# Token-half steps and a scaling product at the two layer ends of a fused two-block kernel

## The chip, the cores and the metric

The kernel runs on one core of one Trainium2 chip. The metric is the device time of one execution in microseconds (us), over 3 runs of the same program. A profiled execution of it gives the trace from which all rows below come; times in rows count from the start of its span.

## What is computed

Two transformer-like blocks run one after the other on 256 tokens of width 2048, in fp32. The parts that matter here are the ends of the two sublayers of the first block: a product with a wide weight, a normalisation over each token's whole row, a residual sum, and a second normalisation whose result feeds the next product.

```python
def rmsnorm(x, g):
    y = xf * lax.rsqrt(jnp.mean(xf * xf, axis=-1, keepdims=True) + RMS_EPS)
    return (y * g.astype(jnp.float32)).astype(x.dtype)

# first_block
x = x + gt_a * rmsnorm(mix @ w_out[l], g_post_attn[l])          # layer end 1
h = rmsnorm(x, g_pre_ffn[l]) * (1.0 + sc_f) + sh_f
f = (jax.nn.silu(h @ w_gate[l]) * (h @ w_up[l])) @ w_down[l]
x = x + gt_f * rmsnorm(f, g_post_ffn[l])                        # layer end 2

# second_block
h = rms_norm(x, norm1_w[l]) * (1.0 + scale[:, None, :]) + shift[:, None, :]
proj = h @ w_in[l] + b_in[l]                                    # begins with v
```

## The kernel before

**Steps.** All wide products are cut into steps of one 128x2048 weight tile (1 MB): SP loads it (`raw`, a ring of 4 buffers), ACT rounds it to `hi` (L243), DVE subtracts (`lo`, L244), and PE multiplies. An fp32 product is three products of rounded parts (L325 to L327), so a step is 4 chunks of 128 input features x 3 products x 2 token halves = 24 matmuls of 128x512. The activations are the stationary side, kept as `khi` and `klo` for each token half `th` (128 tokens). Four steps (`kq` 0 to 3) make one 512-wide output group. `hi` and `lo` have 2 buffers each; an "early" step takes eight 128x512 tiles of the 40-buffer pool `kp` instead, and a "fine" step is converted in 4 or 8 pieces, so that it can start sooner. `run_steps` converts the weights of one step ahead of the step that multiplies.

**Layer end.** The steps of layer end 1 are `wo` (groups `g` 0 to 3), those of layer end 2 the last quarter of the down-projection `dn` (column groups `cg` 0 to 3, two steps each). Each group ends with `z_out`: ACT squares the product and sums it (`jz`, L719), DVE multiplies by a row of gains (L722). That row comes from `row_bcast`: ACT makes eight 128x128 diagonal tiles `dg` (L346), two matmuls spread them over the partitions (`row<-dg,onesr`, L354), DVE multiplies by the gain. After the last group `post_add` takes the root (L330, L331), adds to x (L758), squares again (L760) and takes the second root `r2`. `norm_quad` then handles 128 tokens x 512 features: x is scaled by `r2` (`xs`, L768 on ACT or L770 on DVE), transposed in four PE products against `ident` (`xn`, L773), scaled and shifted per feature (`hn`, L778 and L780, DVE and ACT in turn), and split to `khi` and `klo` (L301, L302). There are 8 quads: 4 for each token half.

**What overlaps.** The last two steps before the end are held and then run token half by token half (24 matmuls of half 0, then 24 of half 1), so the chain of half 0 can run under half 1. The first two steps of the next layer (`gu` after layer end 1, `v` after layer end 2) are held in the same way (`first_steps`); its steps 2 and 3 run both halves together. The engines issue in the order of the program that a scheduler wrote at build time, each engine in order.

Of the kernel before, what the change touches and what calls it, by code (L numbers as in the profile page):

```python
# [12 lines left out]
AF = mybir.ActivationFunctionType  # L13
# [76 lines left out]
def build(tc, A, out):  # L90
# [123 lines left out]
    def run_steps():  # L214
# [3 lines left out]
        fine = {i + d: n for i in barriers for d, n in ((0, 4), (2, 8), (3, 4))}  # L218
        early = {i + 1 for i in barriers}
# [27 lines left out]
        for i in range(n):  # L247
            cur[0] = i
            prep(i)
            prep(i + 1)  # L250
            _, _, fn, _, fill_n, post = steps[i]
            fill(fill_n)
            hi, lo = prepped.pop(i)
            fn(hi, lo)
            for f in pending.pop(i, []):
                f()
            if post is not None:
                post()
# [26 lines left out]
    def group_step(dsts, hi, lo, K, k0, q, nq, last):  # L285
        ks = range(k0 + 4 * q, k0 + 4 * q + 4)
        if last and q == nq - 2:
            held.append((hi, lo))
        elif last and q == nq - 1:
            hi0, lo0 = held.pop()  # L290
            for th in range(2):
                group_mm(dsts, hi0, lo0, K, range(k0 + 4 * q - 4, k0 + 4 * q), nq == 2, False, (th,))
                group_mm(dsts, hi, lo, K, ks, False, True, (th,))
        else:
            group_mm(dsts, hi, lo, K, ks, q == 0, q == nq - 1)
# [255 lines left out]
    MIX = {}  # L551
# [177 lines left out]

    def wo_step(g, kq):  # L730
        def fn(hi, lo):
# [7 lines left out]
            group_step(gacc[g], hi, lo, MIX, 0, kq, 4, g == 3)  # L739
            if kq == 3:  # L740
                p = gacc.pop(g)
                for th in range(2):
                    z_out(g, th, p[th])
# [19 lines left out]

    def norm_quad(th, q, K):
        xs = ttile("xs")
        src = x[:, th, 512 * q:512 * q + 512]
        if q % 2:
            act.activation(xs, src, AF.Copy, scale=r2[:, th:th + 1])  # L768
        else:
            dve.tensor_scalar(xs, src, r2[:, th:th + 1], None, op0=OP.mult)  # L770
        p = at_tile("xn")
        for i in range(4):
            pe.transpose(p[:, i * 128:(i + 1) * 128], xs[:, i * 128:(i + 1) * 128], ident)  # L773
# [9 lines left out]
    def barrier(K):  # L783

        post_add(0)
        norm_quad(0, 0, K)
        norm_quad(0, 1, K)
        post_add(1)

    def first_steps(K, kq, dsts, hi, lo):  # L790

        if kq == 0:
            held.append((hi, lo))
        elif kq == 1:
            ws = [held.pop(), (hi, lo)]
            for th in range(2):
                if th:
                    norm_quad(1, 0, K)
                    norm_quad(1, 1, K)
                for q, (h, l) in enumerate(ws):  # L800
                    group_mm(dsts, h, l, K, range(4 * q, 4 * q + 4), q == 0, False, (th,))
            norm_quad(0, 2, K)
            norm_quad(1, 2, K)
        else:
            group_mm(dsts, hi, lo, K, range(4 * kq, 4 * kq + 4), False, kq == 3)
            if kq == 2:
                norm_quad(0, 3, K)
                norm_quad(1, 3, K)
# [56 lines left out]
    def dn_step(g, cg, q):  # L865
        nq = FGRP[g] // 4

        def fn(hi, lo):
# [9 lines left out]
            group_step(gacc[0], hi, lo, FF, fbase[g], q, nq, g == NG - 1 and cg == 3)  # L878
            if q == nq - 1:
                p = gacc.pop(0)  # L880
                for th in range(2):
# [5 lines left out]
                    if g == NG - 1:  # L887
                        z_out(cg, th, Z[cg, th])
                if g == NG - 1 and cg == 2:
                    preload_sqrt(ssz[:, 2:3])  # L890
# [369 lines left out]
    def wo2_step(g, kq):  # L1260
        def fn(hi, lo):
# [5 lines left out]
            group_step(gacc[g], hi, lo, MG, 0, kq, 4, g == 3)  # L1267
# [123 lines left out]
```

## Time and profile before

| what | us |
|---|---|
| three runs, median (lowest to highest) | 2493.19 (2492.52 to 2494.2) |
| the profiled execution, its time | 2494.39 |
| its span in the trace | 2492.6 |
| PE busy in it | 2415.2 (97%) |
| DVE busy | 1584.0 (64%) |
| ACT busy | 1152.5 (46%) |
| mean granted clock of TensorE | 0.986 of full |

The profiled execution is 1.2 us above the median of the runs. Busy time of PE counts a matmul as long as it occupies the engine, at either of its two clocks, 1.2 and 2.4 GHz (granted 0.5 and 1.00); what PE loses is idle time plus the time at the lower clock.

### The profile page before, as it was taken

How to read it: one execution, taken by the hardware profiler on the slowest of the kernel's cores; microseconds unless marked ns; L12 is line 12 of the kernel's file. 1: busy time of each engine (PE TensorE's matmuls, PEld its weight loads, DVE VectorE, ACT ScalarE, POOL GpSimd, SP SyncE). 2: the span in 40 equal slices, each digit the busy share in tenths (PEclk: the TensorE clock that was granted, in tenths of full speed). 3: DMA queues.
4: the chain of work that ended last, by engine and by line, in shares of the span. 5: the costliest groups of instructions: out<-in, count | busy, mean ns of one | idle time of the engine just before them, and what ended most of it. 6: DMA issues, size and time to landing. Idle time of an engine off the chain costs nothing.

```text
span 2492.6 us, 30211 instructions
## 1 busy us (share of the span) xinstructions
PE 2415.2 (97%) x12444; PEld 2024.2 (81%) x12444; DVE 1584.0 (64%) x1702; ACT 1152.5 (46%) x1394; POOL 0.2 (0%) x4
## 2 busy tenths in 40 slices
PE   6999999979999999999979999999999999999998
PEld 4888888868888888888858888888888888888887
DVE  4888888766666566666664555565456566554555
ACT  5433887553343433334453335455333344344344
POOL 0000000000000000000000000000000000000000
PEclk9999989989999999999989999999999999999999
DMA  8987779937777777677635554555566677555553
GB/s 319 334 334 275 308 282 353 336 126 281 291 271 271 256 284 288 254 284 284 222 122 196 180 195 176 186 177 188 188 213 237 245 250 258 204 200 199 191 195 134
DMA packets 90434, 597.34 MB, mean 240 GB/s; under 512 B 10164, under 2 KB 10804, under 8 KB 20664
## 3 DMA queue, kind: packets, MB, share of 16 engines
q1 hardware_dynamic: 90296, 595.41, 66.0%
q8 instruction: 97, 1.59, 0.3%
q14 instruction: 41, 0.34, 0.0%
HBM read 593.28 MB, written 2.10 MB: 239 GB/s over the span
## 4 chain that ended last, share of the span: by engine, by line
PE 91%; ACT 4%; DVE 3%; DMA 2%; issue 1%; SPq 0%; ACTq 0%; DVEq 0%
PE gu L325 6%; PE gu L326 6%; PE gu L327 6%; PE dn L326 3%; PE dn L327 3%; PE dn L325 3%; PE v L325 2%; PE wo L326 2%; PE wo L325 2%; PE wo L327 2%; PE v L326 2%; PE v L327 2%; DMA graw<-i_ada_k 1%; PE z_a L325 1%; PE ga L325 1%; PE ga L327 1%
## 5 line engine op out<-in xcount | busy, mean ns | idle before, releaser
L244 DVE TENSOR_TENSOR lo<-raw,hi 128x2048 fp32r<-128x2048 f32 (+3 forms) x437 | 927.0, 2124 | 740.2 <-ACT hi L243 739.9
L243 ACT ACTIVATE hi<-raw 128x2048 fp32r<-128x2048 f32 (+3 forms) x437 | 776.9, 1782 | 1057.5 <-PE gu L327 261.1
L325 PE MATMUL gu<-hi,khi 128*128 128x512 f32 x696 | 272.8, 392 | 0.9 <-ACT khi L301 0.9
L326 PE MATMUL gu<-lo,khi 128*128 128x512 f32 x696 | 271.9, 391 | 0.0
L327 PE MATMUL gu<-hi,klo 128*128 128x512 f32 x696 | 271.8, 391 | 0.0
L172 DVE SCALAR_TENSOR_TENSOR graw<-graw,cb 128x2048 f32<-128x2048 f32 x112 | 256.0, 2285 | 16.0 <-DMA graw<-i_w_ada 11.3
L325 PEld LDWEIGHTS gu<-hi,khi 128*128 128x128 f32 x696 | 131.3, 189 | 28.3 <-ACT khi L301 1.1
L327 PEld LDWEIGHTS gu<-hi,klo 128*128 128x128 f32 x696 | 131.3, 189 | 27.5 <-DVE klo L302 0.2
L326 PEld LDWEIGHTS gu<-lo,khi 128*128 128x128 f32 x696 | 131.4, 189 | 27.1
L326 PE MATMUL dn<-lo,khi 128*128 128x512 f32 x352 | 137.3, 390 | 0.2 <-DVE lo L244 0.2
L327 PE MATMUL dn<-hi,klo 128*128 128x512 f32 x352 | 137.0, 389 | 0.0
L325 PE MATMUL dn<-hi,khi 128*128 128x512 f32 x352 | 136.6, 390 | 0.0
L326 PEld LDWEIGHTS dn<-lo,khi 128*128 128x128 f32 x352 | 66.1, 188 | 14.6 <-DVE lo L244 1.0
L325 PEld LDWEIGHTS dn<-hi,khi 128*128 128x128 f32 x352 | 66.1, 188 | 13.8
L327 PEld LDWEIGHTS dn<-hi,klo 128*128 128x128 f32 x352 | 66.1, 188 | 13.7
L281 PE MATMUL qk<-h,lo 128*128 128x256 f32 x256 | 74.1, 290 | 3.1 <-DVE lo L244 3.1
L279 PE MATMUL qk<-h,hi 128*128 128x256 f32 x256 | 75.2, 294 | 0.1
L513 PE MATMUL e<-h,lo 128*128 128x256 f32 x256 | 72.8, 288 | 1.8 <-DVE lo L244 1.8
L511 PE MATMUL e<-h,hi 128*128 128x256 f32 x256 | 73.9, 289 | 0.3 <-ACT gvs L197 0.3
L280 PE MATMUL qk<-h,hi 128*128 128x256 f32 x256 | 73.9, 289 | 0.0
L512 PE MATMUL e<-h,hi 128*128 128x256 f32 x256 | 72.9, 286 | 0.0
L281 PEld LDWEIGHTS qk<-h,lo 128*128 128x128 f32 x256 | 50.6, 197 | 3.5 <-DVE lo L244 3.5
(428 smaller groups left out, 4933.4 us busy)
## 6 DMA issues: line engine op xcount, KB each, us to landing
raw<-i_w_gu SPq DMA_DIRECT2D x88, 1024.0 KB, 4.8
graw<-i_ada_t SPq DMA_DIRECT2D x64, 1024.0 KB, 6.3
graw<-i_w_ada SPq DMA_DIRECT2D x48, 1024.0 KB, 4.8
raw<-i_w_dn SPq DMA_DIRECT2D x44, 1024.0 KB, 4.9
graw<-i_ada_k SPq DMA_DIRECT2D x32, 1024.0 KB, 6.9
raw<-i_w_out SPq DMA_DIRECT2D x32, 1024.0 KB, 4.9
raw<-i_w_s SPq DMA_DIRECT2D x24, 1024.0 KB, 6.8
raw<-i_w_qk SPq DMA_DIRECT2D x16, 1024.0 KB, 7.3
```

Source lines behind the costliest of these rows:

```text
L172: dve.scalar_tensor_tensor(g, g, 1.0, cb, op0=OP.mult, op1=OP.mult, accum_out=dst)
L243: act.activation(hi[:, b:e], r[:, b:e], AF.Copy)
L244: dve.tensor_sub(lo[:, b:e], r[:, b:e], hi[:, b:e].bitcast(F32))
L279: pe.matmul(dst, wh, K[k][:, 0, :], start=s, stop=False)
L280: pe.matmul(dst, wh, K[k][:, 1, :], start=False, stop=False)
L281: pe.matmul(dst, wl, K[k][:, 0, :], start=False, stop=e)
L325: pe.matmul(dsts[th], xh, wh, start=s, stop=False)
L326: pe.matmul(dsts[th], xh, wl, start=False, stop=False)
L327: pe.matmul(dsts[th], xl, wh, start=False, stop=e)
L511: pe.matmul(dst, hv[:, i, c0:c0 + 128], H[k][:, 0, :], start=(k == k0), stop=False)
L512: pe.matmul(dst, hv[:, i, c0:c0 + 128], H[k][:, 1, :], start=False, stop=False)
L513: pe.matmul(dst, lv[:, i, c0:c0 + 128], H[k][:, 0, :], start=False, stop=(k == k1 - 1))
```

## The change

At both layer ends more steps are held and run token half by token half: three before layer end 1 (`wo` group 3, `kq` 1 to 3) and four before layer end 2 (`cg` 2 and 3 of `dn`, two steps each), where it was two; and the first three steps of the next layer, where it was two. More of them are "early" or "fine" to have all their weights at hand, and a new set `late` moves the conversion of the next layer's fourth step behind the products of the third. `row_bcast` stays at the same place in the code, ahead of the step's products, which now are appended to a list there. The scaling by `r2` and the transposing become one product: x itself is the stationary side, and `dx`, the identity scaled by `r2` (one 128x128 DVE instruction for each token half), the moving one, in plain fp32. Three quads of each half run ahead of the first products, the fourth of both halves after them.

```diff
         n = len(steps)
         prepped = {}
         barriers = {i for i, st in enumerate(steps) if st[5] in (barrier1, barrier2)}
-        fine = {i + d: n for i in barriers for d, n in ((0, 4), (2, 8), (3, 4))}
-        early = {i + 1 for i in barriers}
+        fine = {i + d: n for i in barriers for d, n in ((-1, 4), (0, 4), (2, 8), (3, 8))}
+        early = {i + d for i in barriers for d in (-2, 1, 4)}
+        early |= {i - 3 for i, st in enumerate(steps) if st[5] is barrier2}
+        late = {i + 4 for i in barriers}
 
         def prep(i):
             if i >= n or i in prepped:
@@ -247,11 +249,13 @@
...
         for i in range(n):
             cur[0] = i
             prep(i)
-            prep(i + 1)
+            if i + 1 not in late:
+                prep(i + 1)
             _, _, fn, _, fill_n, post = steps[i]
             fill(fill_n)
             hi, lo = prepped.pop(i)
             fn(hi, lo)
+            prep(i + 1)
...
-    def group_step(dsts, hi, lo, K, k0, q, nq, last):
-        ks = range(k0 + 4 * q, k0 + 4 * q + 4)
-        if last and q == nq - 2:
-            held.append((hi, lo))
-        elif last and q == nq - 1:
-            hi0, lo0 = held.pop()
-            for th in range(2):
-                group_mm(dsts, hi0, lo0, K, range(k0 + 4 * q - 4, k0 + 4 * q), nq == 2, False, (th,))
-                group_mm(dsts, hi, lo, K, ks, False, True, (th,))
-        else:
-            group_mm(dsts, hi, lo, K, ks, q == 0, q == nq - 1)
+    def run_held(th):
+        for e in held:
+            group_mm(*e, ths=(th,))
...
-            group_step(gacc[g], hi, lo, MIX, 0, kq, 4, g == 3)
+            e = (gacc[g], hi, lo, MIX, range(4 * kq, 4 * kq + 4), kq == 0, kq == 3)
+            if g == 3 and kq:
+                held.append(e)
+            else:
+                group_mm(*e)
             if kq == 3:
                 p = gacc.pop(g)
+                if g == 3:
+                    run_held(0)
+                    run_held(1)
+                    held.clear()
+                    evac[0] = lambda th: z_out(g, th, p[th])
+                    return
...
+    DX = {}
+
     def norm_quad(th, q, K):
-        xs = ttile("xs")
-        src = x[:, th, 512 * q:512 * q + 512]
-        if q % 2:
-            act.activation(xs, src, AF.Copy, scale=r2[:, th:th + 1])
-        else:
-            dve.tensor_scalar(xs, src, r2[:, th:th + 1], None, op0=OP.mult)
         p = at_tile("xn")
         for i in range(4):
-            pe.transpose(p[:, i * 128:(i + 1) * 128], xs[:, i * 128:(i + 1) * 128], ident)
+            j = 4 * q + i
+            pe.matmul(p[:, i * 128:(i + 1) * 128], x[:, th, j * 128:(j + 1) * 128], DX[th], start=True, stop=True)
...
-        post_add(0)
-        norm_quad(0, 0, K)
-        norm_quad(0, 1, K)
-        post_add(1)
+        for th in range(2):
+            evac[0](th)
+            post_add(th)
+            DX[th] = ttile("dx")[:, 0:128]
+            dve.tensor_scalar(DX[th], ident, r2[:, th:th + 1], None, op0=OP.mult)
+            if th == 0:
+                for q in range(3):
+                    norm_quad(0, q, K)
 
     def first_steps(K, kq, dsts, hi, lo):
 
-        if kq == 0:
-            held.append((hi, lo))
-        elif kq == 1:
-            ws = [held.pop(), (hi, lo)]
-            for th in range(2):
-                if th:
-                    norm_quad(1, 0, K)
-                    norm_quad(1, 1, K)
-                for q, (h, l) in enumerate(ws):
-                    group_mm(dsts, h, l, K, range(4 * q, 4 * q + 4), q == 0, False, (th,))
-            norm_quad(0, 2, K)
-            norm_quad(1, 2, K)
-        else:
-            group_mm(dsts, hi, lo, K, range(4 * kq, 4 * kq + 4), False, kq == 3)
-            if kq == 2:
-                norm_quad(0, 3, K)
-                norm_quad(1, 3, K)
+        e = (dsts, hi, lo, K, range(4 * kq, 4 * kq + 4), kq == 0, kq == 3)
+        if kq == 3:
+            group_mm(*e)
+            return
+        held.append(e)
+        if kq == 2:
+            run_held(0)
+            for q in range(3):
+                norm_quad(1, q, K)
+            run_held(1)
+            held.clear()
+            norm_quad(0, 3, K)
+            norm_quad(1, 3, K)
...
-            group_step(gacc[0], hi, lo, FF, fbase[g], q, nq, g == NG - 1 and cg == 3)
+            e = (gacc[0], hi, lo, FF, range(fbase[g] + 4 * q, fbase[g] + 4 * q + 4), q == 0, q == nq - 1)
+            tail = g == NG - 1 and cg >= 2
+            if tail:
+                held.append(e)
+            else:
+                group_mm(*e)
             if q == nq - 1:
                 p = gacc.pop(0)
-                for th in range(2):
+
+                def finish(th):
                     if g == 0:
                         Z[cg, th] = ztile("zf")
                         act.activation(Z[cg, th], p[th], AF.Copy)
@@ -886,8 +897,19 @@
                         dve.tensor_add(Z[cg, th], Z[cg, th], p[th])
                     if g == NG - 1:
                         z_out(cg, th, Z[cg, th])
+                if not tail:
+                    finish(0)
+                    finish(1)
+                elif cg == 2:
+                    evac[0] = finish
+                else:
+                    before = evac[0]
+                    run_held(0)
+                    run_held(1)
+                    held.clear()
+                    evac[0] = lambda th: (before(th), finish(th))
...
```

The helper `group_step` goes; in the last output product (`wo2`) its two held steps are written out with the same order. The three pieces that follow are the program's order on one engine, in rows as "line operation out<-in shape xcount"; line numbers differ between the two kernels (L773 becomes L778, L325 to L327 become L321 to L323, L354 becomes L350, L346 becomes L342, L243 becomes L245, L719 becomes L715).

PE at layer end 1, before: the last product of `wo`, the transposing products `xn` and the first products of `gu` (`gu_5404` is token half 0, `gu_5405` half 1).

```order
L327 MATMUL wo_5154<-hi,mix 128x512
L773 MATMUL xn<-ident,xs 128x128 x8
L325 MATMUL gu_5404<-khi 128x512
...
L327 MATMUL gu_5404<-hi,klo 128x512
L773 MATMUL xn<-ident,xs 128x128 x8
L325 MATMUL gu_5405<-khi 128x512
L326 MATMUL gu_5405<-klo,khi 128x512
L773 MATMUL xn<-ident,xs 128x128 x3
...
L773 MATMUL xn<-ident,xs 128x128 x13
L325 MATMUL gu_5404<-hi,khi 128x512
```

The same place now, with `gu_5436` and `gu_5437` for the two halves and `gu_5658`, `gu_5659` for the next output group.

```order
L323 MATMUL wo_5166<-hi,mix 128x512
L778 MATMUL xn<-dx,x 128x128 x12
L321 MATMUL gu_5436<-khi 128x512
...
L323 MATMUL gu_5436<-hi,klo 128x512
L778 MATMUL xn<-dx,x 128x128 x12
L321 MATMUL gu_5437<-khi 128x512
L322 MATMUL gu_5437<-klo,khi 128x512
L778 MATMUL xn<-dx,x 128x128 x2
...
L778 MATMUL xn<-dx,x 128x128 x6
L321 MATMUL gu_5658<-hi,khi 128x512
```

Twelve products stand ahead of 36 matmuls of each half where eight stood ahead of 24; of the last quads, two products stand among the matmuls of half 1 and six behind them. The scheduler has put the first steps of the second group (`gu_5658`, `gu_5659`) between them and the fourth step of the first group.

PE ahead of layer end 2, before: the end of `cg` 1, the row of gains, and the first products of `cg` 2 (`dn_9956`).

```order
L327 MATMUL dn_9866<-hi,klo 128x512
L354 MATMUL row<-dg,onesr 128x512 x2
L325 MATMUL dn_9956<-hi,khi 128x512
L326 MATMUL dn_9956<-lo,khi 128x512
L327 MATMUL dn_9956<-hi,klo 128x512
```

Now (`dn_10006` is half 0 of `cg` 2):

```order
L323 MATMUL dn_9892<-hi,klo 128x512
L350 MATMUL row<-dg,onesr 128x512 x4
L321 MATMUL dn_10006<-khi 128x512
L322 MATMUL dn_10006<-klo,khi 128x512
L323 MATMUL dn_10006<-khi,klo 128x512
```

The second pair of row products, which stood behind the 48 matmuls of `cg` 2, stands ahead of all of them.

ACT at that place, before, from the `dg` tiles of that second pair to the layer end:

```order
L719 ACTIVATE jz,ssz<-zf 128x512
L346 ACTIVATE dg<-ident,rhl 128x128 x8
L243 ACTIVATE hi<-raw 128x2048
L719 ACTIVATE jz,ssz<-zf 128x512
L243 ACTIVATE hi<-raw 128x512
L726 ACT_TABLE_LOAD
L726 ACTIVATE pl<-ssz 128x1
```

Now, from the `dg` tiles of the first pair to those of the second:

```order
L342 ACTIVATE dg<-ident,rhl 128x128 x8
L715 ACTIVATE jz,ssz<-zf 128x512
L245 ACTIVATE hi<-raw 128x512 x2
L722 ACT_TABLE_LOAD
L722 ACTIVATE pl<-ssz 128x1
L715 ACTIVATE jz,ssz<-zf 128x512
L236 ACTIVATE khi<-raw 128x512
L245 ACTIVATE hi<-raw 128x512
...
L245 ACTIVATE hi<-raw 128x512
L342 ACTIVATE dg<-ident,rhl 128x128 x8
```

Four pieces of `khi` and four of `hi`, in turn, stand between the second `jz` and the eight `dg`; both `jz` wait for the products of `cg` 1.

## Rows read from the trace of the kernel before

**Rows 1.** Waits of PE over the span: total us, times, longest.

```profile
PE xn L773 <- ACT xs L768: 12.7, 8, 2.8
...
PE xn L773 <- DVE xs L770: 8.4, 2, 5.9
PE gu L325 <- ACT khi L301: 4.3, 3, 2.3
```

**Rows 2.** Timeline, PE, layer end 1: start, us, instruction, [idle before, what ended it].

```profile
507.72 0.39 PE L327 MATMUL wo<-hi,mix 128*128 128x512 f32 x1
510.55 0.66 PE L773 MATMUL xn<-ident,xs 128*128 128x128 f32 x4 [2.45 <-DVE xs L770]
...
515.62 0.80 PE L325 MATMUL gu<-khi 128*128 128x512 f32 x1 [2.29 <-ACT khi L301]
...
523.05 0.60 PE L773 MATMUL xn<-ident,xs 128*128 128x128 f32 x4
524.80 0.66 PE L773 MATMUL xn<-ident,xs 128*128 128x128 f32 x4 [1.16 <-ACT xs L768]
526.53 0.79 PE L325 MATMUL gu<-khi 128*128 128x512 f32 x1 [1.07 <-ACT khi L301]
...
537.47 0.66 PE L773 MATMUL xn<-ident,xs 128*128 128x128 f32 x4 [2.76 <-ACT xs L768]
...
576.20 0.39 PE L327 MATMUL gu<-hi,klo 128*128 128x512 f32 x1
```

**Rows 3.** Timeline, PE, layer end 2, same columns.

```profile
1240.73 0.62 PE L354 MATMUL row<-dg,onesr 128*128 128x512 f32 x2
...
1252.12 0.62 PE L354 MATMUL row<-dg,onesr 128*128 128x512 f32 x2
...
1269.80 1.11 PE L773 MATMUL xn<-ident,xs 128*128 128x128 f32 x4 [5.93 <-DVE xs L770]
...
1301.04 0.80 PE L325 MATMUL v<-hi,khi 128*128 128x512 f32 x1 [0.46 <-ACT khi L301]
...
1335.28 0.39 PE L327 MATMUL v<-hi,klo 128*128 128x512 f32 x1
```

**Rows 4.** Stretches: us, PE busy (instructions), PEclk granted, DMA share, GB/s.

```profile
507.95:576.40 68.45, 55.42 (x225) 0.88 0.38 139
510.55:519.57 9.02, 5.49 (x17) 0.62 0.12 25
1241.19:1335.50 94.31, 79.20 (x323) 0.87 0.40 141
281.00:287.00 6.00, 4.12 (x33) 1.00 0.46 185
407.00:413.00 6.00, 4.00 (x57) 1.00 0.99 384
```

**Rows 5.** Timeline, PE, attention: plain fp32 products (two records each) and transposing ones.

```profile
268.77 0.39 PE L632 MATMUL o<-v,ptS 128*128 128x128 f32 x2
269.00 0.49 PE L619 MATMUL pt<-ident,sm 128*128 128x128 f32 x3
269.32 0.60 PE L568 MATMUL s<-rot 128*128 128x256 f32 x2
```

**Rows 6.** Timeline, PE: plain fp32 products at the lower clock.

```profile
340.48 0.63 PE L569 MATMUL s<-rot,qm 128*128 128x128 f32 x2
340.90 1.11 PE L568 MATMUL s<-rot,qm 128*128 128x256 f32 x2
```

**Rows 7.** Timeline, ACT, ahead of layer end 2.

```profile
1240.41 0.63 ACT L719 ACTIVATE jz<-zf 128x512 f32<-128x512 f32 x1 [2.96 <-DVE zf L886]
...
1243.45 2.44 ACT L346 ACTIVATE dg<-ident,rhl 128x128 fp32r<-128x128 f32 x8
...
1253.06 1.28 ACT L726 ACT_TABLE_LOAD   x1
...
1255.07 1.66 ACT L243 ACTIVATE hi<-raw 128x512 fp32r<-128x512 f32 x3
1256.64 2.18 ACT L234 ACTIVATE khi<-raw 128x512 fp32r<-128x512 f32 x4
```

**Rows 8.** Timeline, ACT, layer end 1.

```profile
502.71 0.60 ACT L719 ACTIVATE jz<-wo 128x512 f32<-128x512 f32 x1 [1.68 <-PE wo L327]
...
508.25 0.57 ACT L719 ACTIVATE jz<-wo 128x512 f32<-128x512 f32 x1
```

More of the change, by code (lines that the diff above doesn't have):

```diff
@@ L728, in build @@
     ROWS = ((0, 1), (1, 1), (2, 0), (3, 0))
+    evac = [None]
     def wo_step(g, kq):
@@ L888, in fn @@
                         z_out(cg, th, Z[cg, th])
+                if not tail:
[9 more added lines that the diff above has]
+                    evac[0] = lambda th: (before(th), finish(th))
                 if g == NG - 1 and cg == 2:
-                    preload_sqrt(ssz[:, 2:3])
+                    preload_sqrt(ssz[:, 1:2])
         return fn
@@ L1266, in fn @@
                 gacc[g] = [acc_tile("wo0"), acc_tile("wo1")]
-            group_step(gacc[g], hi, lo, MG, 0, kq, 4, g == 3)
+            e = (gacc[g], hi, lo, MG, range(4 * kq, 4 * kq + 4), kq == 0, kq == 3)
+            if g == 3 and kq > 1:
+                held.append(e)
+            else:
+                group_mm(*e)
+            if g == 3 and kq == 3:
+                run_held(0)
+                run_held(1)
             if kq == 1:
```

## Prediction

> **What bounds the kernel now.** PE does: it is busy 97% of the span, so only its idle time and its time at the lower clock can be won. I read first the list of its waits [rows 1]. Two entries lead in the middle of the program, both at the transposing products of the layer ends: 12.7 us behind the ACT scaling and 8.4 us behind the DVE scaling, then 4.3 us of the first `gu` products behind `khi`. The timeline shows where they lie. At layer end 1 the last `wo` product starts at 507.72, so its slot ends at 507.95; then come waits of 2.45 and 2.29 us around the first quads, 1.16 and 1.07 around those of half 1, 2.76 at the last quads [rows 2]. At layer end 2 the same pattern begins with a wait of 5.93 us [rows 3]. The windows show the second loss: from 510.55 to 519.57 the granted clock averages 0.62, and over all of 507.95 to 576.40 it is 0.88 [rows 4]. 576.43 is when 192 products of the first two `gu` groups are done (the last starts at 576.20), 1335.51 when 192 of `v` are.
>
> **Prices.** A 128x512 product at the full clock: between the two pairs of row products at 1240.73 and 1252.12 lie 48 products and one pair, 11.39 / 50 = 0.228 us [rows 3]. 192 of them, eight weight steps, take 43.7 us. A plain fp32 product of 128x128 shows as two records and takes 0.23 us from start to start (268.77 to 269.00); a transposing one 0.32 / 3 = 0.107 [rows 5]. At the lower clock the plain one takes 0.42 [rows 6].
>
> **The change, part 1: layer end 1.** In the trace 68.5 us pass from 507.95 to 576.43. After the change:
> - 192 products, 43.7 us.
> - 32 plain fp32 products instead of 32 transposing ones: 32 x 0.23 = 7.4 us on PE, at the lower clock 13.4 (the transposing ones, 32 x 0.107 = 3.4 us, are part of the old 68.5). Taking the scaled copies `xs` off ACT and DVE costs nothing elsewhere; one 128x128 DVE instruction `dx` replaces the first of them in the chain.
> - The chain of half 0. In the trace `jz` starts at 502.71 [rows 8] and the first transposing product at 510.55 [rows 2], 7.8 us later. Now 36 products of half 1 stand beside it where 24 did, 8.2 us instead of 5.5, so the roots are there when the last of them ends. That removes the 2.45 us; bounds 0 to 1 us left over.
> - Half 0, from products to `gu`: 12 products last 2.8 us. In the trace the first `gu` follows the start of a pair of quads by 3.5 us (523.05 to 526.53) [rows 2]. The first quad's `hn`, `khi` are done some 3.5 us after the start, and ACT, by its order, still has some pieces of `hi` to convert when the products start, so about 1.2 us are idle.
> - Half 1: its `jz` stands on ACT behind the three `khi` of half 0. It starts some 6.5 us after half 0's products began, and its chain (7.8 us in the trace, 6.4 here with no weight pieces between) ends about 1.0 us after the 36 products of half 0. Then 12 products, and again some 1.5 us until the first `khi`.
> - The last quads: their products lie among or behind those of half 1, and 24 products of the next weight step follow (5.5 us), which hide a chain of 3.5 us. The 2.76, and what follows it in the trace, fall away. If that cover failed, the same 2.76 would come back.
>
> Idle time is so 1.2 + 1.0 + 1.5 = 3.7 us; nearest rows bound it by 0 and by the waits of today (2.45 + 2.29 + 1.16 + 1.07 = 7.0). The clock I take as full: stretches with a third of the time idle in shorter waits had a granted clock of 1.00 (busy 4.12 and 4.00 of 6 us) [rows 4], and here a wait never exceeds 1.5 us with 2.8 us of products beside it. Sum: 43.7 + 7.4 + 3.7 = 54.8 us, a gain of 13.7.
>
> **Part 2: layer end 2.** From 1241.19 to 1335.51 pass 94.3 us today, with 96 `dn` products first. After the change I see a **new wait**, in the order of the program and in no row. The second pair of row products moves ahead of all products of `cg` 2, on PE in order. It needs the second set of `dg`, and on ACT these stand behind the table load, the two `jz` of `cg` 1 and eight conversion pieces. In the trace the first `jz` of `cg` 1 starts at 1240.41; its input should come 0.8 us earlier, since DVE's pieces ahead of it are shorter (an estimate), so 1239.6. From there, by rows of the same instructions [rows 7]: `jz` 0.6, two `hi` pieces 1.1 (1.66 / 3 each), table load 1.3, its use and the second `jz` 0.75, eight pieces x 0.55 = 4.4, eight `dg` 2.45: 1250.2. PE is done with the first row pair at 1241.19, so it idles **9.2 us** with the release. Queued behind it on PE are all 96 `dn` products. Bounds: 0, if the dg tiles were ready as today, and 15 us if two weight transfers had to land in between as well. After the wait the clock is low for a while: at 515.62, after 2.29 us of waiting and transposing before, products ran 3.95 us at half the clock (to 519.57, inside the stretch of 0.62), which cost 2.0; I take 2.3, bounds 0 and 3.
>
> Then 96 products (21.9), the row pair 0.46, 192 products 43.7, scaling products 7.4, and idle time as at layer end 1, 3.7. Half 0's chain has 48 products of half 1 as cover, 10.9 us against 7.8. Sum: 9.2 + 2.3 + 21.9 + 0.5 + 43.7 + 7.4 + 3.7 = 88.7 us against 94.3, a gain of 5.6.
>
> **Sum.** 13.7 + 5.6 = 19.3 us. Against the profiled execution's own 2494.39 that is 2475.1. Since the profiled one lies 1.2 above the median of the runs shown, the median comes to 2473.9; I say 2474. Edits that I cost at nothing: `late` and the `early` and `fine` sets (DVE and ACT convert the same bytes; DVE is 64% and ACT 46% busy), the written-out `wo2` steps (same order).
>
> **Rivals.**
> - *No dg wait.* If the eight `dg` were done by 1241, the 9.2 and the 2.3 go: 2474 - 11.5 = 2462.5. For it: today's `dg` for that pair are done at 1245.9, well ahead of their use at 1252.12. Against it: the order of ACT, where pieces that wait for nothing later stand ahead of them.
> - *The clock falls at the small waits.* Each time it falls costs what it cost at 515.62, 2.0 us; up to two more at each end: 2474 + 8 = 2482. For it: at 526.53, after waits of 1.16 and 1.07 us with eight transposing products between, the clock was low again (part of the 0.88) [rows 2, 4]. Against: the plain products fill more of the time between than the transposing ones did.
>  The Trainium skill (TensorE: Matmul & The Clock Gate, Part 4: PE-mode transpose) says that transposing products do not bring the clock to its full rate. By that rule plain products in their place would keep it up, and the time would be the 2474 of the main case. The trace agrees in part: the eight transposing products from 510.55 stand in the stretch of 0.62, but four at 523.05 took 0.60 us, against 1.11 for four at 1269.80.
> - *The other side: the clock stays at half through the token-half stretches.* 36 + 36 products at each end, and 96 more of `dn` after the 9.2 us wait, 240 in all, with plain fp32 products and short waits between them. Each at the lower clock costs 0.2 us more, and each scaling product 0.42 - 0.23. The whole would be 240 x 0.2 + 64 x 0.19 = 60 us, so from a third of it on (19 us) the gain is gone; at half of it, 30 us, the time is 2474 + 30 = 2504. Against it: today the clock came back after 3.95 us of products at 515.62, and the whole 94.3 us of layer end 2 had a granted clock of 0.87 [rows 4].
> - *The change does nothing.* Then the waits would be the same chain at a new place: `jz` of half 1 now comes later, after the `khi` of half 0. If the waits of today (7.0 at each end, plus 5.93 and 2.76) all came back, and the dg wait too, 2474 + 3.3 + 3.3 + 2 x 2.76 + 2 x 2 = 2490, within 0.2%.
>
> **How the numbers follow.** 0.2% is 5 us, about what a measurement of this kernel can tell from no change: faster means under 2488, slower over 2498. Chances: main case 0.50 (2468 to 2480), no dg wait 0.20 (2460 to 2466), clock falls 0.20 (2480 to 2487), nothing 0.05, other side 0.05. Faster 0.90, same 0.05, slower 0.05. The range takes in the first rival and most of the second: 2462 to 2484.
>
> **What would show it.** In the trace of the changed kernel: the list of waits of PE should have no `xn` behind a scaling, a wait of 8 to 10 us of the row product (L350) behind `dg` (L342) at about 1227 (1241 less the gain of layer end 1), the clock low for some us behind it, and waits of 1 to 1.5 us at `xn` behind `dx` and at the first `gu` and `v` behind `khi`. Plain products should be 0.23 us apart. From the last `wo` product to the 192nd of `gu` some 55 us should pass. I am wrong if the dg wait is missing, if the clock is low over more than a few us at layer end 1, or if the weights of the fourth step come late (a wait of `gu` or `v` for `hi` or `lo`), since `late` converts them only behind the third step's products.

## The result and the profile after

The changed kernel takes 2476.19 us (median of 4 runs, 2475.55 to 2478.41), the kernel before beside it 2493.69 (2492.52 to 2495.04): a ratio of 0.9931, 95% interval 0.9914 to 0.9948. The forecast was 2474 within 2462 to 2484. The profiled execution took 2476.79 us with a span of 2475.0, so it is set against the 2492.6 of before: 17.6 us shorter.

The list of PE's waits, with total, times and longest, has the new wait, and the waits of the layer ends' `xn` for `xs` are gone [rows 1]; the two larger entries of the list, cut here, lie in the early part of the kernel:

```profile
...
PE row L350 <- ACT dg L342: 8.2, 1, 8.2
...
PE v L321 <- ACT khi L297: 2.7, 2, 1.4
PE gu L321 <- ACT khi L297: 2.5, 2, 1.4
PE xn L778 <- DVE dx L794: 2.3, 2, 1.4
...
PE dn L322 <- DVE lo L246: 1.5, 2, 0.8
```

The timeline of PE at layer end 1 answers to [rows 2]. A scaling product leaves two records, so x24 is twelve products:

```profile
506.27 2.84 PE L778 MATMUL xn<-dx,x 128*128 128x128 f32 x24
510.18 0.53 PE L321 MATMUL gu<-khi 128*128 128x512 f32 x1 [1.07 <-ACT khi L297]
...
519.85 2.94 PE L778 MATMUL xn<-dx,x 128*128 128x128 f32 x24 [0.95 <-DVE dx L794]
524.21 0.50 PE L321 MATMUL gu<-khi 128*128 128x512 f32 x1 [1.42 <-ACT khi L297]
...
524.78 0.61 PE L778 MATMUL xn<-dx,x 128*128 128x128 f32 x4
...
532.99 1.50 PE L778 MATMUL xn<-dx,x 128*128 128x128 f32 x12
534.24 0.71 PE L321 MATMUL gu<-hi,khi 128*128 128x512 f32 x2
```

The scaling products start at 506.27, right behind the last `wo` product, and three waits are left: 1.07, 0.95 and 1.42 us. The last quads (524.78 and 532.99) have no wait. The 192nd `gu` product starts at 561.55. On ACT the chain of half 1 begins with its square:

```profile
512.68 0.59 ACT L715 ACTIVATE jz<-wo 128x512 f32<-128x512 f32 x1
```

At layer end 2 the timeline of PE [rows 3] begins with the wait for `dg`:

```profile
1227.65 0.63 PE L350 MATMUL row<-dg,onesr 128*128 128x512 f32 x2
1236.51 1.22 PE L350 MATMUL row<-dg,onesr 128*128 128x512 f32 x2 [8.23 <-ACT dg L342]
1237.53 0.63 PE L321 MATMUL dn<-khi 128*128 128x512 f32 x1
```

On ACT the timeline shows what stands ahead of it, in the order that the forecast added up [rows 7]:

```profile
1226.37 0.62 ACT L715 ACTIVATE jz<-zf 128x512 f32<-128x512 f32 x1
...
1228.14 1.28 ACT L722 ACT_TABLE_LOAD   x1
...
1229.55 0.61 ACT L715 ACTIVATE jz<-zf 128x512 f32<-128x512 f32 x1
...
1230.16 0.61 ACT L236 ACTIVATE khi<-raw 128x512 fp32r<-128x512 f32 x1
...
1234.32 2.43 ACT L342 ACTIVATE dg<-ident,rhl 128x128 fp32r<-128x128 f32 x8
```

The windows show the clock [rows 4]; columns are us, PE busy with instructions, granted clock, DMA share, GB/s:

```profile
506.27:561.77 55.50, 52.07 (x257) 1.00 0.46 171
...
1236.51:1241.37 4.86, 4.86 (x12) 0.50 0.94 389
1241.37:1317.42 76.05, 71.84 (x345) 1.00 0.34 120
```

Layer end 1 runs at the full clock throughout; 4.9 us behind the wait for `dg` run at half of it, and the rest of layer end 2 at the full one.

Two lengths compare kernels better than whole times do: from the start of the last `wo` product to that of the 192nd `gu` product (end 1), and from the last product of `cg` 1 to the 192nd of `v` (end 2). The start of end 1 differs from kernel to kernel by up to 5 us (506.0 to 511.3). A part of it lies in PE's waits for transfers (`gv` behind `graw`), which add up to 9.9 to 15.2 us by kernel. Each length below is worked out from the starts of these products in the trace of that kernel.

| kernel | end 1, us | end 2, us | median us (runs), before beside it |
|---|---|---|---|
| before | 68.5 | 94.8 | 2493.69 (4) |
| changed | 55.5 | 89.8 | 2476.19 (4), 2493.69 |
| dg_early | 55.5 | 78.8 | 2468.29 (4), 2492.51 |
| row_after_half0 | 55.5 | 79.3 | 2469.64 (4), 2492.51 |
| product_twice | 59.6 | 92.8 | 2482.16 (4), 2492.51 |
| before_with_product | 66.7 | 91.1 | 2492.75 (8), 2492.51 |
| no_late | 58.6 | 91.0 | 2483.94 (6), 2493.29 |
| two_first_steps | 59.3 | 95.0 | 2488.15 (7), 2493.29 |
| scale_and_transpose | 61.0 | 94.2 | 2485.83 (8), 2493.29 |
| dg_early_evac1 | 54.3 | 77.8 | 2466.94 (4), 2493.29 |
| scale_plain_product | 61.5 | 95.5 | 2489.68 (8), 2491.20 |

Of the 17.6 us, 13.0 come from end 1 (68.5 to 55.5) and 5.0 from end 2 (94.8 to 89.8). The profiled execution of the changed kernel also reached end 1 1.7 us earlier, lost 1.6 between the two ends and 0.4 behind the second. Between the ends PE waits twice for `lo` (1.5 us in the list above): on DVE that `lo` stands behind a `graw` instruction which waited for its transfer. Whether the change brings this wait about stays open: product_twice and scale_and_transpose, whose code is the same between the ends, don't have it, and their stretch is 0.5 us shorter than before; experiment 4, without the longer hold, has it (1.6 us).

### The profile page after: what moved, and what is told of

Read it like the earlier page. It is cut to its first block, busy times and chain, and to the rows that moved or that the text cites. A ratio compares the mean times of both kernels' runs of the same rounds, so it can differ in the third digit from the quotient of the medians.

```text
span 2475.0 us, 30384 instructions
## 1 busy us (share of the span) xinstructions
PE 2410.0 (97%) x12508; PEld 2023.7 (82%) x12508; DVE 1584.8 (64%) x1727; ACT 1151.2 (47%) x1415; POOL 0.2 (0%) x4
## 4 chain that ended last, share of the span: by engine, by line
PE 89%; DVE 4%; ACT 3%; DMA 3%; issue 1%; SPq 0%; ACTq 0%; DVEq 0%
PE gu L322 6%; PE gu L321 6%; PE gu L323 6%; PE dn L322 3%; PE dn L323 3%; PE dn L321 3%; PE wo L322 2%; PE wo L321 2%; PE wo L323 2%; PE v L321 2%; PE v L322 2%; PE v L323 2%; DVE lo L246 2%; DMA graw<-i_ada_k 2%; PE z_a L321 1%; PE ga L321 1%
## 5 line engine op out<-in xcount | busy, mean ns | idle before, releaser
L246 DVE TENSOR_TENSOR lo<-raw,hi 128x2048 fp32r<-128x2048 f32 (+3 forms) x446 | 917.1, 2061 | 715.2 <-ACT hi L245 714.9
L245 ACT ACTIVATE hi<-raw 128x2048 fp32r<-128x2048 f32 (+3 forms) x446 | 769.1, 1730 | 1037.2 <-PE gu L323 251.3
L321 PE MATMUL gu<-hi,khi 128*128 128x512 f32 x688 | 268.3, 390 | 0.0
L323 PE MATMUL gu<-hi,klo 128*128 128x512 f32 x688 | 267.7, 389 | 0.0
L323 PEld LDWEIGHTS gu<-hi,klo 128*128 128x128 f32 x688 | 129.2, 188 | 26.7
L321 PEld LDWEIGHTS gu<-hi,khi 128*128 128x128 f32 x688 | 129.1, 188 | 26.5
L322 PE MATMUL dn<-lo,khi 128*128 128x512 f32 x336 | 131.0, 390 | 1.5 <-DVE lo L246 1.5
L323 PE MATMUL dn<-hi,klo 128*128 128x512 f32 x336 | 130.8, 389 | 0.0
L321 PE MATMUL dn<-hi,khi 128*128 128x512 f32 x336 | 130.5, 390 | 0.0
L322 PEld LDWEIGHTS dn<-lo,khi 128*128 128x128 f32 x336 | 63.1, 188 | 15.2 <-DVE lo L246 2.4
L323 PEld LDWEIGHTS dn<-hi,klo 128*128 128x128 f32 x336 | 63.1, 188 | 13.2
L321 PEld LDWEIGHTS dn<-hi,khi 128*128 128x128 f32 x336 | 63.1, 188 | 13.1
```

What stands on the lines that cost most here:

```text
L245: act.activation(hi[:, b:e], r[:, b:e], AF.Copy)
L246: dve.tensor_sub(lo[:, b:e], r[:, b:e], hi[:, b:e].bitcast(F32))
L321: pe.matmul(dsts[th], xh, wh, start=s, stop=False)
L322: pe.matmul(dsts[th], xh, wl, start=False, stop=False)
L323: pe.matmul(dsts[th], xl, wh, start=False, stop=e)
```

## The experiments

**1. dg_early.** Is the wait for `dg` a plain loss?

```diff
-                i = 0 if (cg, q) == (0, 0) else cg + 1 if q == nq - 1 else 4
+                i = {(0, 0): 0, (0, nq - 1): 1, (1, 0): 3, (1, nq - 1): 2}.get((cg, q), 4)
```

> The changed kernel with one edit: the fourth row of gains is begun two steps earlier (cg 1, first step, instead of cg 2, second step), so its eight dg tiles stand ahead of the table load on ACT. Theory: the 8.2 us wait of the row product and some 2 us of lower clock behind it are a plain loss on PE, so the time falls by about 10 us, from 2476.2 to 2466, and layer end 2 (from the first row pair to the 192nd product of v) takes 79.4 us instead of 89.5. Rival: the wait covers other late work (the conversion of the four held steps, the chain of half 0), which then shows as waits of dn for hi or lo or of xn for dx, and the time falls by less than 5 us, to 2471 or more.

(The tiles are begun at the first step of `cg` 1, three steps earlier than at the second step of `cg` 2; the expectation counts two.)

Measured 2468.29 us (2465.36 to 2471.9), ratio 0.9903 (0.9886 to 0.9919). End 2 is 11.0 us shorter than in the changed kernel. The whole fell by less, 9.4 us by the profiled executions and 7.9 by the medians: outside the ends 1.7 us were lost, where among others `gv` waits longer for `graw` (13.8 us in all, against 10.8). The windows from the row products to the last `dn`, and from there to the 192nd `v`, show no half clock and no idle PE in the first:

```profile
1229.34:1251.86 22.52, 22.52 (x99) 1.00 0.59 218
1251.86:1308.10 56.24, 52.01 (x258) 1.00 0.39 141
```

On ACT the `dg` now stand ahead of the table load:

```profile
1226.26 2.44 ACT L342 ACTIVATE dg<-ident,rhl 128x128 fp32r<-128x128 f32 x8
...
1229.85 1.28 ACT L722 ACT_TABLE_LOAD   x1
```

The 8.2 us and what the clock costs behind them were pure loss; the rival (the wait covers other late work) falls, since no other wait of the layer ends grew (`v` and `gu` for `khi` 2.7 and 2.5 us, `xn` for `dx` 2.3, as in the changed kernel).

**2. row_after_half0.** The same on PE alone, with ACT's order as it is.

```diff
+    row_end = {}
-    def row_bcast(c16, g, grow, key):
+    def row_bcast(c16, g, grow, key, keep=False):
...
-        later(0, end)
+        if keep:
+            row_end[0] = end
+        else:
+            later(0, end)
...
-                    row_bcast(gt1, i, A["g_post_ffn"], i)
+                    row_bcast(gt1, i, A["g_post_ffn"], i, keep=(i == 3))
...
                     run_held(0)
+                    row_end.pop(0)()
```

> The changed kernel with the dg tiles left where they stand on ACT, and only the two row products moved on PE: behind the 48 products of half 0 of the held dn steps instead of ahead of all 96. Theory: 48 products (10.9 us) cover the 8.2 us for which dg is late, so the same 10 us are won as with earlier dg tiles, 2466, unless the row of gains now ends the chain of half 0 later, by at most 1 us. Rival: ACT itself is the bound here, since the tiles that stand behind dg (weights of the first v steps) are late as well; then less than 5 us are won.

Measured 2469.64 us (2465.88 to 2473.0), ratio 0.9906 (0.9891 to 0.992); end 2 is 79.3 us, 0.5 more than in experiment 1. The `dg` still end late, and the second row pair runs without a wait behind the 48 products:

```profile
1239.37 2.44 ACT L344 ACTIVATE dg<-ident,rhl 128x128 fp32r<-128x128 f32 x8
```

```profile
1232.69 0.62 PE L352 MATMUL row<-dg,onesr 128*128 128x512 f32 x2
...
1244.38 0.62 PE L352 MATMUL row<-dg,onesr 128*128 128x512 f32 x2
```

So the order on PE alone is enough to remove the loss: ACT had `dg` ready 2.6 us before they were needed here (1241.8 against 1244.38).

**3. product_twice.** What does a scaling product cost?

```diff
+            for _ in range(2):
-            pe.matmul(p[:, i * 128:(i + 1) * 128], x[:, th, j * 128:(j + 1) * 128], DX[th], start=True, stop=True)
+                pe.matmul(p[:, i * 128:(i + 1) * 128], x[:, th, j * 128:(j + 1) * 128], DX[th], start=True, stop=True)
```

> The changed kernel with every scaling product done twice into the same place, 64 products of 0.227 us more. Theory: the waits for the first khi after each group of twelve (1.07 and 1.42 us, 1.31 and 1.42 at layer end 2) take up part of it, the rest lies on PE: 2.7 - 1.1 and 2.7 - 1.4 us and 1.8 for the last quads, 4.7 us at each end, 2486 in all. Rival: all of it is on the path, 14.5 us, 2491. Second rival: plain fp32 products bring the clock down, more than 2495.

Measured 2482.16 us (2481.29 to 2484.87), ratio 0.9958 (0.9943 to 0.9973). Timeline of PE at end 1:

```profile
506.31 5.52 PE L779 MATMUL xn<-dx,x 128*128 128x128 f32 x48
...
521.10 5.62 PE L779 MATMUL xn<-dx,x 128*128 128x128 f32 x48 [1.06 <-DVE dx L795]
...
534.76 3.74 PE L779 MATMUL xn<-dx,x 128*128 128x128 f32 x32
```

The `gu` product behind the first of these rows, and the window of end 1:

```profile
511.58 0.47 PE L321 MATMUL gu<-khi 128*128 128x512 f32 x1
```

```profile
506.31:565.85 59.54, 58.48 (x321) 1.00 0.44 160
```

24 products take 5.5 us, 0.23 each, so the price is right. The waits for the first `khi` are gone, taken up by the second products as the theory says; end 1 grows by 4.1 and end 2 by 3.0 us (4.7 each expected; why they grow by less was not followed up). The rival in which all 14.5 us lie on the path falls, and the clock stays full at end 1.

**4. before_with_product.** The product alone, in the kernel before.

```diff
         post_add(0)
+        make_dx(0)
         norm_quad(0, 0, K)
         norm_quad(0, 1, K)
         post_add(1)
+        make_dx(1)
```

(`make_dx` and the product in `norm_quad` are those of the change, but that `dx` lies in another buffer.)

> The kernel before with the scaling product alone: two held steps on both sides as before, no xs, dx as moving side. Theory: the gain comes from the longer covers, and the product takes away only the waits for xs on ACT (1.24, 1.16, 2.76, 1.16 us at each end) and gives some of it back at khi and as longer products, so the time is 2485 to 2490. Rival: the product is what wins, and the time falls to about 2480.

Measured 2492.75 us (2488.35 to 2496.64), ratio 1.0 (0.9989 to 1.001): no change in the whole, so both the 2485 to 2490 of the theory and the 2480 of the rival were missed. The ends are 1.8 and 3.7 us shorter; its profiled execution reached end 1 3.6 us later than that of the kernel before and lost 1.7 between the ends, 1.4 of it in waits of `dn` for `lo` (1.6 us against 0.2). Why these parts, which the edit doesn't touch, are longer stays open. The timeline at end 1:

```profile
513.96 2.05 PE L774 MATMUL xn<-dx,x 128*128 128x128 f32 x16 [2.25 <-DVE dx L768]
518.45 0.50 PE L325 MATMUL gu<-khi 128*128 128x512 f32 x1 [2.44 <-ACT khi L301]
...
544.06 0.80 PE L325 MATMUL gu<-hi,khi 128*128 128x512 f32 x1 [3.23 <-ACT khi L301]
```

The waits for `xs` are gone, and part of the time turns up again: `dx` is waited for as the first `xs` was (2.25 us, 2.45 before), and the waits of `gu` for `khi` add up to 7.7 us instead of 4.3.

**5. no_late.** What does the set `late` do?

```diff
-        late = {i + 4 for i in barriers}
+        late = set()
```

> The changed kernel with an empty set late: the fourth step of the next layer is converted ahead of the third step's products again. By the order of the program its 24 products then stand right behind the products of the last quads, and the next group's step no longer lies between. Theory: that step is the cover of the last quads, so a wait of 2.5 to 3.5 us for khi appears at each end, with the clock lower for a while behind it (2 us): 8 to 11 us in all, about 2485. Rival: late only spreads the conversions, and the time stays within 2 us of 2476.

Measured 2483.94 us (2483.3 to 2490.49), ratio 0.9967 (0.9955 to 0.998). End 1 is 3.1 us and end 2 1.2 us longer, but not where the theory had it:

```profile
523.37 4.57 PE L778 MATMUL xn<-dx,x 128*128 128x128 f32 x24 [2.12 <-DVE dx L794]
...
529.92 1.95 PE L778 MATMUL xn<-dx,x 128*128 128x128 f32 x16
```

The last quads (529.92) run among the products of half 1, and no wait for `khi` follows them. What grew is the wait for `dx`, 0.95 to 2.12 us (and 1.38 to 2.57 at end 2), and behind it the twelve products took 4.57 us instead of 2.94, at half the clock in part. Here conversions of the fourth step (`klo<-raw`) stand within half 1's chain, on DVE between its first root and the addition to x:

```profile
516.93 1.28 DVE L237 TENSOR_TENSOR klo<-raw,khi 128x512 fp32r<-128x512 f32 x2
...
518.20 0.67 DVE L237 TENSOR_TENSOR klo<-raw,khi 128x512 fp32r<-128x512 f32 x1
518.79 2.07 DVE L766 SCALAR_TENSOR_TENSOR x<-z,r,x 128x512 f32<-128x512 f32 x3
```

That the whole came near the expected 2485 is luck: the theory had the mechanism wrong, and the ends give only 4.3 of the 7.2 us between the two profiled executions.

**6. two_first_steps.** Two first steps half by half instead of three.

```diff
-        if kq == 3:
+        if kq > 1:
...
-        if kq == 2:
+        if kq == 1:
             run_held(0)
-            for q in range(3):
+            for q in range(2):
                 norm_quad(1, q, K)
...
+            norm_quad(0, 2, K)
+            norm_quad(1, 2, K)
```

(The last quads follow the third step's products, as before; half 0 has two quads ahead.)

> The changed kernel with two first steps of the next layer run half by half (24 products each) instead of three; held steps before the end and the scaling product as changed. Theory: 24 products cover the chain of half 1 less well than 36 (2.7 us less, of which the wait for dx grows by 1.5 to 2.7), and the third quads of both halves lose their cover (a wait of about 3 us for khi): with the clock 4 to 7 us at each end, 2484 to 2490. Rival: the held steps before the end are what gains, and the time stays at 2476 to 2479.

Measured 2488.15 us (2482.92 to 2492.03), ratio 0.9978 (0.9965 to 0.9991). The ends are 3.8 and 5.2 us longer. Timeline of PE at end 1:

```profile
512.08 0.57 PE L321 MATMUL gu<-khi 128*128 128x512 f32 x1 [2.20 <-ACT khi L297]
...
520.28 2.05 PE L778 MATMUL xn<-dx,x 128*128 128x128 f32 x16 [0.81 <-DVE dx L794]
524.34 0.50 PE L321 MATMUL gu<-khi 128*128 128x512 f32 x1 [2.00 <-ACT khi L297]
...
534.87 0.50 PE L322 MATMUL gu<-lo,khi 128*128 128x512 f32 x1 [0.73 <-DVE lo L246]
```

The window behind the first of these waits, and the same wait at end 2:

```profile
512.08:515.60 3.52, 3.52 (x9) 0.54 0.54 175
```

```profile
1270.45 0.50 PE L321 MATMUL v<-khi 128*128 128x512 f32 x1 [2.20 <-ACT khi L297]
```

The size fits, the places only in part: with eight products instead of twelve ahead of `khi`, the waits there are 2.20 and 2.00 us instead of 1.07 and 1.42. The wait of 3 us for the third quads didn't come (0.73, for `lo`), and the wait for `dx` grew at end 2 alone (2.43 us). Behind the first wait of 2.20 us the clock fell (0.54 over the next 3.5 us); behind the wait of 2.20 at end 2 it did not. The edit shortens the covers and the group of products ahead of `khi` at once, and no run separates the two.

**7. scale_and_transpose.** The scaling product undone, the covers kept.

```diff
+        xs = ttile("xs")
+        src = x[:, th, 512 * q:512 * q + 512]
+        if q % 2:
+            act.activation(xs, src, AF.Copy, scale=r2[:, th:th + 1])
+        else:
+            dve.tensor_scalar(xs, src, r2[:, th:th + 1], None, op0=OP.mult)
...
-            pe.matmul(p[:, i * 128:(i + 1) * 128], x[:, th, j * 128:(j + 1) * 128], DX[th], start=True, stop=True)
+            pe.transpose(p[:, i * 128:(i + 1) * 128], xs[:, i * 128:(i + 1) * 128], ident)
```

> The changed kernel with the scaling product undone: xs on DVE and ACT in turn and transposing products, all covers as changed. Theory: the 64 products cost 7 us less on PE, the waits for xs and khi around the first quads of each half take most of it back, and the clock falls once or twice at each end, 2 us each: 2474 to 2484. Rival: without the plain product the waits of the kernel before return (1.2 us behind each xs on ACT) and most of the gain is lost, more than 2486. Second rival: the product is a loss, the time falls below 2472.

Measured 2485.83 us (2479.72 to 2494.05), ratio 0.9971 (0.9958 to 0.9985). The ends are 5.5 and 4.4 us longer, between the theory's 2484 and the first rival's 2486. Timeline and window of end 1:

```profile
511.48 0.66 PE L783 MATMUL xn<-ident,xs 128*128 128x128 f32 x4 [0.84 <-DVE xs L780]
...
522.56 0.66 PE L783 MATMUL xn<-ident,xs 128*128 128x128 f32 x4 [1.81 <-DVE xs L780]
524.38 2.30 PE L783 MATMUL xn<-ident,xs 128*128 128x128 f32 x8 [1.16 <-ACT xs L778]
...
539.63 0.66 PE L783 MATMUL xn<-ident,xs 128*128 128x128 f32 x4 [2.52 <-ACT xs L778]
```

```profile
508.23:569.26 61.03, 53.33 (x226) 0.92 0.44 156
```

The waits for `xs` are back, the 2.5 us at the last quads too, and the clock is 0.92 instead of 1.00.

**8. scale_plain_product.** Is it the wait for `xs` or the kind of product that lowers the clock? As experiment 7, but with the plain product of `xs` and the identity.

```diff
-            pe.transpose(p[:, i * 128:(i + 1) * 128], xs[:, i * 128:(i + 1) * 128], ident)
+            pe.matmul(p[:, i * 128:(i + 1) * 128], xs[:, i * 128:(i + 1) * 128], ident, start=True, stop=True)
```

> As scale_and_transpose (x scaled to xs on DVE and ACT first), but the product is the plain fp32 one with xs as stationary side and the unscaled identity as moving side. Theory A: what the scaling product won in the changed kernel is the wait for xs; the waits of 1.2 to 2.5 us behind xs stay, the clock falls behind them as in scale_and_transpose, and the layer ends take 61 to 64 us and 94 to 97 us. Theory B: the kind of product keeps the clock up; the waits stay but no stretch at half the clock follows them at layer end 1, and it takes 58 to 60 us.

Measured 2489.68 us (2487.21 to 2492.23), ratio 0.9988 (0.9976 to 0.9999); ends 61.5 and 95.5 us, as theory A has it. The timeline at end 1:

```profile
509.36 1.16 PE L783 MATMUL xn<-ident,xs 128*128 128x128 f32 x8 [1.23 <-ACT xs L778]
511.53 1.82 PE L783 MATMUL xn<-ident,xs 128*128 128x128 f32 x8 [1.01 <-DVE xs L780]
```

```profile
507.08:568.60 61.52, 55.68 (x258) 0.94 0.44 154
```

Eight records took 1.16 us at 509.36 and 1.82 at 511.53: the clock fell behind plain products too, here behind waits of 1.23 and 1.01 us between them, and over the whole of end 1 it is 0.94 (0.92 in experiment 7). The waits are not quite those of experiment 7: `xn` waits for `xs` 12.1 us in all, against 14.8 there.

**9. dg_early_evac1.** Both findings put to use: `dg` early, and the squares of half 1 ahead of the second quad of half 0.

```diff
+        evac[0](0)
+        make_dx(0)
+        norm_quad(0, 0, K)
+        evac[0](1)
+        norm_quad(0, 1, K)
+        norm_quad(0, 2, K)
+        make_dx(1)
```

(`make_dx` is `post_add` and the `dx` instruction; the loop over `th` goes. The edit of experiment 1 is made as well.)

> Two edits: the dg tiles earlier as in dg_early, and the squares and gains of half 1 (jz) are put ahead of the second quad of half 0 at both ends. Theory: jz of half 1 stands behind the three khi of half 0 on ACT, which causes the waits for dx (0.92 and 1.37 us); they go, and the first khi of half 0 comes at most 0.6 us later: 1 to 2 us below dg_early, and its layer ends become 54.6 to 55.2 and 77.2 to 78.2 us long (55.5 and 78.8 there). Rival: jz ahead delays the khi of half 0 by as much as it wins, no change.

Measured 2466.94 us (2464.99 to 2470.27), ratio 0.9896 (0.9876 to 0.9916). The whole times of this and of experiment 1 can't be told apart. The ends can: 54.3 and 77.8 us, 1.2 and 1.0 shorter, a little more than expected at end 1. Timeline of PE there:

```profile
513.66 0.53 PE L321 MATMUL gu<-khi 128*128 128x512 f32 x1 [1.07 <-ACT khi L297]
...
522.25 2.85 PE L778 MATMUL xn<-dx,x 128*128 128x128 f32 x24
```

The wait for `dx` is gone at end 1 (0.44 us are left at end 2), and the first `khi` comes no later than before: 1.07 us.

## Why the prediction was right, step by step

- **End 1, 54.8 us forecast, 55.5 measured.** The three waits were forecast as 1.2, 1.0 and 1.5 us and came as 1.07, 0.95 and 1.42. The chain of half 0 lies under the 36 products of half 1 and leaves no wait. The 1.0 us came out right with a chain that was put too short: from its `jz` to the scaling products of half 1 pass 7.2 us (512.68 to 519.85), where 6.4 were forecast, and the forecast's own terms (6.5 + 6.4 less 2.8 + 1.2 + 8.2) give 0.7. The missing 0.7 us is not in the waits; the first products behind a wait start further apart than the 0.228 us of the sum: the first three last from 510.18 to 511.24, which alone is 0.4 us more.
- **End 2, 88.7 us forecast, 89.3 measured** between the same bounds (from the end of the first row pair's slot to that of the 192nd `v` product, 1228.11 to 1317.42). The wait for `dg` was shorter than forecast, the other idle time longer: 4.1 us (2.7 for `khi`, 1.4 for `dx`) where 3.7 were forecast.
- **The price of a scaling product, 0.23 us.** Twelve took 2.84 us in the change and 24 took 5.52 in experiment 3.
- **The wait for dg, 9.2 us forecast, 8.2 measured.** The chain on ACT was right to a few tenths in its terms: first `jz` forecast at 1239.6, which with the 13.1 us by which this place moved (1240.73 to 1227.65) is 1226.5, measured 1226.37. The last `dg` was forecast 10.6 us after that `jz` began and ended 10.4 after it (1236.75), and the row product starts 0.24 us ahead of that modelled end. The list also counts the idle time from the modelled end of the first pair (1227.65 + 0.63), 0.17 us behind the slot that the forecast counted from. One term of this chain comes from an edit that the cut diff above doesn't show: the instruction that brings the table for the square root in early (`preload_sqrt`) reads a sum of `cg` 1 instead of `cg` 2, so the table load (1.28 us) now stands ahead of these `dg`, where it stood behind them [rows 7]. Experiments 1 and 2 show by two ways that this wait, and nothing behind it, cost 10.5 to 11.0 us with the clock; the forecast had 11.5.
- **The clock.** Behind the `dg` wait 4.86 us at half the clock, so 2.4 us lost against 2.3 forecast. Elsewhere at the ends it stayed full, so the rival in which it falls at the small waits didn't come true. The prediction's ground for this was weaker than it says: its two stretches of 1.00 have not several shorter waits but one each, of 1.82 us (before `qk`, at 285.6) and of 2.00 (before `gv`, at 411.8), with dense products on both sides. Experiments 5 to 8 show where it would have: at waits of 2.12, of 2.20, of 1.81 and 1.16, and of 1.23 and 1.01 us close together. In experiment 8 the products were plain ones, and it fell nevertheless; in experiment 7 the first twelve transposing products, with waits of 1.16 and 0.84 us between them, stayed at the full clock (four in 0.66 us at 511.48). Putting plain products in the place of transposing ones did not bring the time back (61.0 to 61.5 us): by the forecast's prices the 32 plain ones are 3.9 us longer, and nearly as much was won in waits and time at the lower clock. The page of the Trainium skill that the prediction named (TensorE: Matmul & The Clock Gate, Part 4: PE-mode transpose) says that transposing products do not bring the clock to its full rate. What the prediction drew from it, that plain products would keep the clock up, is not borne out by experiment 8; the page's rule by itself no run here tests.
- **Where the working was off.** It worked out the state with both edits and left open what each gives alone; the expectation of experiment 4 then gave the covers nearly all of the gain. The runs show the two as partners at end 1: the covers without the product win 7.5 and 0.6 us at the ends (experiment 7 against before, the `dg` wait included at end 2), the product without the covers 1.8 and 3.7 (experiment 4), both together 13.0 and 5.0. At end 1 the two alone make 9.3 of the 13.0 us; at end 2 they make 4.3 of the 5.0 and nearly add up. The prediction's total was right because it worked out the state with both. No run takes back the longer hold ahead of the ends by itself. Experiments 4 and 6 side by side bear out what the prediction said of it: with two held steps the first scaling products wait 2.25 and 5.73 us for `dx`, with the longer hold and only two first steps they don't wait.
- **`late` at nothing** was wrong. Without it the ends are 3.1 and 1.2 us longer (experiment 5), since the fourth step's conversions then delay `dx` of half 1. The step that I named as cover of the last quads is not needed for it: in experiment 5 they lie under the products of half 1 alone. The `early` and `fine` sets, costed at nothing as well, no run takes back.
- **The total.** At the ends 18.0 us were won where 19.3 were forecast. The parts outside the ends, which the forecast left alone, changed by 1.7 us one way and 2.0 the other; that they cancel, so that the whole came to 17.6, is luck.

Of the rivals, "no dg wait" is what experiments 1 and 2 build: it was priced at 2462.5 and measured at 2468.3 and 2469.6, beside a kernel before of 2492.5. In dg_early the two ends together are 29.0 us shorter than before, close to the 30.8 of that rival's sum, and the whole of the profiled execution 27.0 (24.2 by the medians): 2.0 us were lost outside the ends. The rival of half clock throughout is out, since the clock is 1.00 over end 1, and so is that of no change. The prediction's own sign of being wrong, a late fourth step, didn't show either: `gu` and `v` wait for no `hi` or `lo` at the layer ends.

## What to carry to other kernels

When products are held back to be run later, look at what else is issued at the place where they used to be: a small product that waits for another engine moves to the front of the queue, and everything held waits with it. Waits of one chain can be worth more removed together than one at a time, since a wait removed alone may turn up again at the next link: 1.8 and 7.5 us alone, 13.0 together at end 1 here. Compare stretches between fixed instructions as well as whole times: here kernels that are the same up to end 1 (the changed one, experiments 1 and 2) reached it at 506.0 to 510.9 us.

## What the runs showed that was not expected

- The clock followed the kind of product less than the waits between: full with twelve plain products and single waits of up to 1.42 us (the changed kernel's end 1), half behind plain products with waits of 1.23 and 1.01 us, 1.2 us apart (experiment 8). What decides behind which waits it falls stays open: in experiment 6 it fell behind one wait of 2.20 us and not behind another.
- When the fourth step's weights are converted, though the same bytes are converted either way, was worth 3.1 us at end 1 (experiment 5): 1.2 of it as wait and 1.6 as products at half the clock.
